# Spreading the gate projections and two branch products through the RWKV stage, and inverting blocks of 32 instead of 16

## The chip, the cores and the metric

The kernel runs on one core of one Trainium2 chip. The metric is the device time of one execution in microseconds (us). TensorE (PE) does the matrix products, VectorE (DVE), ScalarE (ACT) and GpSimd (POOL) the elementwise work; SyncE (SP) and ACT issue most of the DMAs. An engine works through its own queue in the order in which the program was written.

## The reference, cut to what matters

The whole is two transformer-like blocks on 512 latent and 256 context tokens of width 1024. The change lies in the first block's mixer. It has three branches of width 512 (pooling, differential attention, a bidirectional RWKV recurrence), whose products with `w_br` are gated and summed:

```python
w_log = -softplus(-(w0 + einsum('bldr,drc->bldc', tanh(wl), w2))) - 0.5
decay = exp(-exp(w_log)) ...
def wkv_step(S, inp):                      # one token; scanned forwards and backwards
    r, w, k, v, a, b = inp
    sa = einsum('dbhvk,dbhk->dbhv', S, a)
    S = S * w[..., None, :] + sa[..., None] * b[..., None, :] + v[..., None] * k[..., None, :]
    return S, einsum('dbhvk,dbhk->dbhv', S, r)

def merge_branches(branches, gates, w_br, w_out):
    g = sigmoid(gates.reshape(B, L, N_BRANCH, D_MODEL))
    merged = g[:, :, 0] * (branches[0] @ w_br[0])
    for n in range(1, N_BRANCH):
        merged = merged + g[:, :, n] * (branches[n] @ w_br[n])
    return merged @ w_out
```

The kernel does the recurrence in chunks of 128 tokens. That needs the inverse of a unit triangular 128x128 matrix per chunk, head and direction (a matrix I - A, A strictly triangular). It inverts small diagonal blocks row by row on VectorE and joins them by doubling (16 to 32 to 64 to 128) on TensorE, then corrects the result once.

## The kernel before, in words

**Order of the work.** All instructions go through a thin wrapper (`Engine`, so nearly all rows carry line L355, the wrapper's). A class `Clock` keeps a rough model of the engines while the program is written. `weave` (line 1361) takes several generators ("streams"), each with a rank; it runs next the stream whose announced time has come, lowest rank first. If the modelled recent activity of TensorE is under `LOW`, streams of rank 2 go first: these are fillers. What comes out is a fixed order on every engine.

**The first stage** (`phase1`, line 738) weaves four streams: `rwkv_inputs`, `attend` and `rwkv_blocks` of rank 0, and `pools_gates` of rank 2, which ends with the filler `ada_steps` (products with the `ada` weights, matmuls named `ada`). `rwkv_inputs` goes through four column chunks c of the branch. Each ends by transposing the gathered 32x32 blocks (`blkT<-blk`, `rwkv_chunk_inputs`) and putting a job on `todo`; `rwkv_blocks` takes it up. `rwkv_block` (line 1329) inverts two 16x16 blocks of every 32x32 block at a time, in 15 steps i of one multiplication (`blt<-inv,blkT`, 2·i·i elements) and one sum (`inv<-blt`) on DVE. Between steps it yields: for 1 us of modelled TensorE time in chunks 0 to 2 (`PACE`), for none in chunk 3, whose job comes last, beside the end of attention. Two transposes (`blkO`) and four stores to `rw_inv` end it.

**The RWKV stage** (`rwkv`, line 1386) has 24 units and 24 steps (4 column chunks times 6 token chunks). Two generators `units` of rank 1 prepare units, at most `AHEAD` = 3 ahead; two generators `steps` of rank 0, for two column chunks at a time, carry the state S through. `rwkv_unit` loads the operands and `rw_inv` (tile X), makes the masked products (matmuls `m`, tiles Mt, Mh, Ml, Ah, Al), then goes three times through the level loop (line 1488): matmuls `pg`, DVE mask G, matmuls `pT` and `pZ`, DVE additions into TZ (the last turn writes T and has no `pZ`). Then come `pZt`, `pR`, `pf`, and last the pair Zh, Zl. `rwkv_step` does the products `pc`, `pw`, `py` with Rs, Us and S on ACT and DVE between them. `rwkv_out` normalises a finished column chunk and stores it to `rw_out`.

The filler of this stage is `gates` (line 782): 24 projections of the latent tokens (matmuls `gp<-h1l_...`), each in two halves of 12 matmuls of 512 columns, with the weights split into a high part on ACT (`wgh`) and a low part on DVE (`wgl`), then a tanh on ACT and a store to `gates`. Nothing holds it back but its rank.

**The merge stage** (`merge`, line 1110) goes over the branches b = 0, 1, 2. It loads a branch from HBM (`brt<-pooled`, `attended`, `rw_out`), splits it, and for each of 8 output tiles n loads a weight unit (`wr<-w_br`) and a gate (`bgt<-gates`), does 12 matmuls of 512 columns, multiplies by the gate on DVE (`mt`, one buffer; for b = 0 into `mg` itself) and, for b = 1 and 2, adds to `mg` on POOL. Then `mg` is halved and split, and 8 tiles of the `w_out` product follow. Loads of expert weights (`ew<-w_exp`) for the next stage are issued in between on SP.

Of the kernel before, what the change touches and what calls it, by code (L numbers as in the profile page):

```python
# [30 lines left out]
NL, NCX = 512, 256  # L31
# [124 lines left out]
def _tables():  # L156
# [261 lines left out]
class Builder:  # L418
# [288 lines left out]
    def phase1(self, es):  # L707
# [12 lines left out]
        self.d_g = dt("gates", [3, 8, 128, NL])  # L720
        self.d_br = [dt(n, [4, 128, NL]) for n in ("pooled", "attended", "rw_out")]
        self.fac = self.pool(es, "keep1").tile([128, 4, 2, 6, 2], FT, name="fac")
        with ExitStack() as e:
            hl = self.pool(e, "h1l")
# [57 lines left out]
    def gates(self, es, which, tag, ahead, kc, **k):  # L782
# [6 lines left out]
        for b, n in at:  # L789
# [4 lines left out]
            yield self.after(t)  # L794

# [314 lines left out]
    def merge(self, es):  # L1110
# [5 lines left out]
        acc = mp.tile([128, 8, NL], FT, name="mg")  # L1116
        halves = lambda: [wp.tile([128, 4, NL], FR, name=n, tag=n) for n in ("br_hi", "br_lo")]
        for b in range(3):
            bh, bl = halves()
            for c in range(4):  # L1120
                t = wp.tile([128, NL], FT, name="brt", tag="brt")
                nc.scalar.dma_start(t, self.d_br[b][c])
                self.split(bh[:, c], bl[:, c], t)
            for n in range(8):
                t = wp.tile([128, NL], FT, name="bgt", tag="bgt", bufs=3)
                nc.scalar.dma_start(t, self.d_g[b, n])
                (y,) = self.gemm_fm(self.wunit(D["w_br"], (b * 8 + n) * 512 * 128, 4, 128, ring), 0, 4, [(bh, bl, 0, NL)])

                o = acc[:, n] if b == 0 else wp.tile([128, NL], FT, name="mt", tag="mt", bufs=1)
                nc.vector.scalar_tensor_tensor(o, t, 1.0, y, op0=OP.add, op1=OP.mult)  # L1130
                if b:
                    nc.gpsimd.tensor_add(acc[:, n], acc[:, n], o)
                yield
# [37 lines left out]
    def rwkv_inputs(self, es):  # L1171
# [25 lines left out]
        inv = wp.tile([128, 33, 32], FT, name="inv")  # L1197
        nc.gpsimd.memset(inv, 0.0)
        nc.gpsimd.memset(inv[:, :32].rearrange("p i j -> p (i j)")[:, 0::33], 1.0)
# [12 lines left out]
    def rwkv_chunk_inputs(self, c, proj, pp, W, blk, inv):  # L1212
# [102 lines left out]
        A = pp.tile([128, 33, 32], FT, name="blkT", tag="blkT")  # L1315
        nc.vector.transpose(A[:, :32], blk)
# [14 lines left out]

# [1599 lines left out]
```

## Time and profile before

| | us |
|---|---|
| median of 3 runs | 4079.49 |
| lowest and highest | 4067.55 and 4089.53 |
| profiled execution, whole time | 4074.84 |
| its span | 4073.0 |
| PE, DVE, ACT, POOL busy | 3729.5, 2439.1, 1579.8, 530.0 |

A busy time adds up the instructions of an engine; instructions that overlap a little in the pipeline are united in the share. The chain that ended last is 57% PE and 8% DVE. The granted clock of TensorE has two levels, 1.2 and 2.4 GHz, and is given as a share of the higher: 1.00 or 0.50, or a mean of the two over a stretch. A matmul's duration holds its time in the pipeline, so throughput is read from the distance between the starts of neighbouring matmuls. In a row of a timeline, [1.44 <-DVE Rs] means that the engine sat idle for 1.44 us before it, and that DVE's write of Rs ended that.

The stages that the change touches lie at about 115 to 660 us (first stage), 660 to 1344 us (RWKV stage) and 1344 to 1484 us (merge stage: products until 1431 us, then `w_out`).

### The profile page before, as it was taken

How to read it: one execution, taken by the hardware profiler on the slowest of the kernel's cores; microseconds unless marked ns; L12 is line 12 of the kernel's file. 1: busy time of each engine (PE TensorE's matmuls, PEld its weight loads, DVE VectorE, ACT ScalarE, POOL GpSimd, SP SyncE). 2: the span in 40 equal slices, each digit the busy share in tenths (PEclk: the TensorE clock that was granted, in tenths of full speed). 3: DMA queues.
4: the chain of work that ended last, by engine and by line, in shares of the span. 5: the costliest groups of instructions: out<-in, count | busy, mean ns of one | idle time of the engine just before them, and what ended most of it. 6: DMA issues, size and time to landing. Idle time of an engine off the chain costs nothing.

```text
span 4073.0 us, 50718 instructions
## 1 busy us (share of the span) xinstructions
PE 3729.5 (92%) x18620; PEld 2905.8 (71%) x18620; DVE 2439.1 (60%) x4500; ACT 1579.8 (39%) x2765; POOL 530.0 (13%) x750
## 2 busy tenths in 40 slices
PE   8998987998898779999998999899999999999998
PEld 4775435887787667666665887587888887667886
DVE  5577776767776558888874566545323335445444
ACT  3332333332222237666663554223312324434342
POOL 0222211212221221111100000110100100000010
PEclk9998998996556879999999999999999999999999
DMA  5225663321100729998964334411111210012322
GB/s 188 94 94 190 212 226 105 99 95 36 43 27 17 264 76 367 335 340 330 333 256 162 110 122 145 151 32 57 63 63 63 83 63 27 13 42 81 100 93 88
DMA packets 213183, 537.97 MB, mean 132 GB/s; under 512 B 41282, under 2 KB 63459, under 8 KB 186436
## 3 DMA queue, kind: packets, MB, share of 16 engines
q1 hardware_dynamic: 172240, 461.38, 32.8%
q10 hardware_dynamic: 36852, 61.79, 4.4%
q0 software_dynamic: 3840, 11.54, 0.9%
q8 instruction: 148, 2.42, 0.2%
q14 instruction: 103, 0.84, 0.1%
HBM read 486.38 MB, written 48.24 MB: 131 GB/s over the span
## 4 chain that ended last, share of the span: by engine, by line
PE 57%; DVE 8%; ACT 2%; DMA 2%; issue 2%; POOL 1%; another core or an unknown queue 0%; ACTq 0%; SPq 0%; DVEq 0%; POOLq 0%
PE gp L355 33%; PE eg L355 5%; PE ed L355 3%; DVE el L355 2%; PE S L355 2%; PE vp L355 1%; PE eT L355 1%; PE o L355 1%; PE cp L355 1%; PE pc L355 1%; PE fk L355 1%; ACT eh L355 1%; PE py L355 1%; PE hy L355 1%; PE mw L355 1%
## 5 line engine op out<-in xcount | busy, mean ns | idle before, releaser
L355 ACT CAST wh<-wr 128x512 fp32r<-128x512 f32 (+5 forms) x306 | 199.6, 675 | 599.2 <-PE gp L355 538.6
L355 PE MATMUL gp<-h_hi,wh 128*128 128x512 f32 (+1 forms) x1128 | 402.0, 360 | 6.4 <-ACT h_hi L355 3.8
L355 DVE TENSOR_TENSOR el<-ew,eh 128x1024 fp32r<-128x1024 f32 x284 | 354.2, 1273 | 58.4 <-ACT eh L355 56.7
L355 PE MATMUL gp<-h_lo,wh 128*128 128x512 f32 (+1 forms) x1128 | 386.8, 357 | 0.5 <-DVE h_lo L355 0.3
L355 DVE TENSOR_TENSOR wl<-wr,wh 128x512 fp32r<-128x512 f32 (+5 forms) x306 | 228.0, 764 | 245.0 <-ACT wh L355 244.2
L355 PE MATMUL gp<-h_hi,wl 128*128 128x512 f32 (+1 forms) x1128 | 344.1, 357 | 0.0
L355 ACT CAST eh<-ew 128x1024 fp32r<-128x1024 f32 x288 | 292.9, 1048 | 18.8 <-PE ec L355 12.9
L355 PEld LDWEIGHTS gp<-h_hi,wh 128*128 128x128 f32 x1128 | 212.8, 190 | 56.6 <-ACT h_hi L355 7.4
L355 PEld LDWEIGHTS gp<-h_lo,wh 128*128 128x128 f32 x1128 | 213.7, 190 | 34.0 <-DVE h_lo L355 2.3
L355 PEld LDWEIGHTS gp<-h_hi,wl 128*128 128x128 f32 x1128 | 190.5, 191 | 16.7 <-DVE wl L355 0.3
L355 PE MATMUL ada<-wada,adas 128*32 128x512 f32 (+1 forms) x576 | 162.8, 651 | 29.3 <-DMA wada<-ada_w 16.2
L355 PE MATMUL gp<-z_hi,wh 128*128 128x512 f32 (+1 forms) x528 | 187.8, 356 | 0.0
L355 PE MATMUL eg<-el,xg 128*128 128x512 f32 x384 | 161.8, 421 | 27.6 <-DVE el L355 27.4
L355 PE MATMUL gp<-z_lo,wh 128*128 128x512 f32 (+1 forms) x528 | 179.1, 354 | 0.0
L355 PE MATMUL eg<-eh,xg 128*128 128x512 f32 x384 | 176.2, 459 | 0.1
L355 PE MATMUL gp<-z_hi,wl 128*128 128x512 f32 (+1 forms) x528 | 158.8, 355 | 0.0
L355 POOL MEMSET cvb<- 128x1 f32 x170 | 9.6, 98 | 1061.2 <-DVE fg L355 691.4
L355 PE MATMUL gp<-h_lo,wih 128*128 128x256 f32 (+1 forms) x384 | 131.4, 342 | 0.0
L355 PE MATMUL gp<-h_hi,wih 128*128 128x256 f32 (+1 forms) x384 | 128.1, 354 | 0.0
L355 PEld LDWEIGHTS eg<-el,xg 128*128 128x128 f32 x384 | 72.4, 189 | 69.9 <-DVE el L355 50.9
L355 PE MATMUL eg<-ew,xw 128*128 128x512 f32 x256 | 120.2, 592 | 0.0
L355 PEld LDWEIGHTS gp<-z_hi,wh 128*128 128x128 f32 x528 | 99.1, 188 | 22.7
(849 smaller groups left out, 9670.5 us busy)
## 6 DMA issues: line engine op xcount, KB each, us to landing
ew<-w_exp SPq DMA_DIRECT2D x192, 1024.0 KB, 6.8
wada<-ada_w SPq DMA_DIRECT2D x192, 256.0 KB, 4.2
wr<-ffn_up SPq DMA_DIRECT2D x176, 256.0 KB, 2.6
wada<-w_ada_b SPq DMA_DIRECT2D x64, 256.0 KB, 4.3
wg<-w_in_a SPq DMA_DIRECT2D x48, 256.0 KB, 2.6
wi<-w_in SPq DMA_DIRECT2D x48, 256.0 KB, 2.7
wr<-ffn_dn SPq DMA_DIRECT2D x32, 384.0 KB, 3.1
wr<-ffn_dn SPq DMA_DIRECT2D x32, 320.0 KB, 3.3
```

Of the source, the lines that this page charges most:

```text
L355: return f(*a, **k)
```

## The change

Two edits. First, `rwkv_block` inverts each 32x32 block whole, in 31 steps with i·i elements each, and the level loop starts at 32, so that it has two turns instead of three. Second, the filler of the RWKV stage becomes `filler`: the 24 gates, then for the branches 0 and 1 the 16 products that `merge` did, with their loads, splits, gating and (for b = 1) additions; the sum goes to HBM as `merged`. The filler may only go as far as the steps that are done allow: item j of 64 (a gate counts two, a product one) waits until j ≤ 64·(done/24 + 0.1). `merge` loads `merged` (2 MB) and does branch 2 alone, with the addition on DVE and two buffers for `mt`. The latent operand `h1l` moves to the other side of SBUF so that its space can be given to the products.

```diff
-    for i in range(4, 7):                     # _tables: masks of the levels
+    for i in range(5, 7):
-    def gates(self, es, which, tag, ahead, kc, **k):
+    def gates(self, es, which, tag, ahead, kc, pace=None, **k):
-        for b, n in at:
+        for i, (b, n) in enumerate(at):
+            while pace and 2 * i > self.FILL * pace():
+                yield self.later()
+    FILL = 64
+    def filler(self, pace):
+        with ExitStack() as e:
+            yield from self.gates(e, range(self.GATES_A, 24), "g", 2, 4, pace, side="right")
+        self.h1s.close()
+        with ExitStack() as e:
+            yield from self.merge_first(e, pace)
+    def merge_first(self, es, pace):
...
+        feed = Feed(self, wp, "b", [units[i] for i in range(16)], 2)
+        for b in range(2):
...
+            for c in range(4):
+                t = wp.tile([128, NL], FT, name="mbt", tag="mbt")
+                nc.sync.dma_start(t, self.d_br[b][c])
+                yield self.after(t)
+                self.split(bh[:, c], bl[:, c], t)
+            for n in range(8):
+                while 48 + 8 * b + n > self.FILL * pace():
+                    yield self.later()
+                t = wp.tile([128, NL], FT, name="mgt", tag="mgt", bufs=2)
+                nc.sync.dma_start(t, self.d_g[b, n])
+                if b:
+                    a = wp.tile([128, NL], FT, name="mga", tag="mga")
+                    nc.sync.dma_start(a, self.d_mg[:, n])
+                H, L = feed.next()
+                yield max(self.after(H, L, bh, bl), self.room("g"))
+                y = self.ps("mp", "g")
+                for k in range(4):
+                    self.gemm_k([y], H, L, k, [(bh, bl, 0, NL)], k == 0, k == 3)
+                nc.vector.scalar_tensor_tensor(t, t, 1.0, y, op0=OP.add, op1=OP.mult)
+                if b:
+                    nc.gpsimd.tensor_add(t, t, a)
+                nc.scalar.dma_start(self.d_mg[:, n], t)
+                yield
     def merge(self, es):
+        nc.scalar.dma_start(acc, self.d_mg)
-        for b in range(3):
...                                            # the body for b = 2 alone, and:
+            o = wp.tile([128, NL], FT, name="mt", tag="mt")
+            nc.vector.scalar_tensor_tensor(o, t, 1.0, y, op0=OP.add, op1=OP.mult)
+            nc.vector.tensor_add(acc[:, n], acc[:, n], o)
     def rwkv_block(self, c, pp, A, inv):
-        for i in range(1, 16):
-            t = pp.tile([128, 2, 15, 15], FT, name="blt", tag="blt")[:, :, :i, :i]
-            nc.vector.tensor_mul(t, I2[:, :, :i, :i].rearrange("p g m j -> p g j m"), A2[:, :, i, None, :i].to_broadcast([128, 2, i, i]))
-            nc.vector.tensor_reduce(I2[:, :, i, :i], t, op=OP.add, axis=AX.X)
+        for i in range(1, 32):
+            t = pp.tile([128, 31, 31], FT, name="blt", tag="blt")[:, :i, :i]
+            nc.vector.tensor_mul(t, inv[:, :i, :i].rearrange("p m j -> p j m"), A[:, i, None, :i].to_broadcast([128, i, i]))
+            nc.vector.tensor_reduce(inv[:, i, :i], t, op=OP.add, axis=AX.X)
     def rwkv(self, es):
-        self.weave(*gens, (2, self.gates(es, range(self.GATES_A, 24), "g", 2, 4)))
+        self.weave(*gens, (2, self.filler(lambda: done[0] / 24 + 0.1)))
     def rwkv_unit(self, c, n, up, q, P):
-        for lv in (4, 5, 6):
+        for lv in (5, 6):
```

## Rows read from the trace of the kernel before

**Rows 1.** The page's 40 slices of the span: granted clock in tenths.
```profile
PEclk9998998996556879999999999999999999999999
```

**Rows 2.** Stretches: length, busy us (x instructions) by engine, clock, DMA share, GB/s.
```profile
core 0: us, PE busy (x) PEld busy (x) DVE busy (x) ACT busy (x) POOL busy (x), PEclk, DMA share, GB/s
240.00:363.00 123.00, 113.73 (x587) 85.77 (x585) 86.02 (x180) 37.03 (x64) 29.18 (x30) 0.93 0.41 137
363.00:494.00 131.00, 123.93 (x544) 64.08 (x543) 95.32 (x224) 45.60 (x108) 23.10 (x29) 0.97 0.63 214
494.00:606.00 112.00, 100.75 (x427) 46.27 (x425) 87.78 (x211) 38.26 (x91) 21.41 (x20) 0.92 0.67 225
606.00:660.00 54.00, 33.61 (x102) 17.45 (x102) 30.64 (x91) 14.17 (x38) 2.73 (x3) 0.69 0.17 50
...
721.00:906.00 185.00, 173.87 (x1100) 148.63 (x1100) 128.49 (x217) 66.86 (x129) 35.13 (x49) 1.00 0.28 91
906.00:1319.00 413.00, 350.00 (x1927) 328.72 (x1927) 304.60 (x569) 107.58 (x213) 97.09 (x113) 0.61 0.11 35
...
1344.00:1431.00 87.00, 71.74 (x301) 56.96 (x301) 46.48 (x68) 28.23 (x47) 27.28 (x16) 0.93 0.80 279
```

**Rows 3.** Timeline of PE: start us, duration us, engine, instruction, count, idle before.
```profile
898.15 0.40 PE L355 MATMUL gp<-h1l_lo,wgh 128*128 128x512 f32 x1
...
900.48 0.40 PE L355 MATMUL gp<-h1l_hi,wgl 128*128 128x512 f32 x1
...
902.52 0.28 PE L355 MATMUL pR<-T,Al 128*128 128x128 f32 x1
...
903.19 0.28 PE L355 MATMUL pR<-T,Al 128*128 128x128 f32 x1
...
909.40 0.44 PE L355 MATMUL pc<-Rs,Zh 128*128 128x128 f32 x1 [1.44 <-DVE Rs L355]
...
1144.93 0.41 PE L355 MATMUL pR<-T,Al 128*128 128x128 f32 x1
...
1146.21 0.41 PE L355 MATMUL pR<-T,Al 128*128 128x128 f32 x1
```

**Rows 4.** Timeline of DVE: the last write (Zl) of units 1, 8 and 24.
```profile
720.65 1.29 DVE L355 TENSOR_TENSOR Zl<-Zt,Zh 128x512 fp32r<-128x512 f32 x1
...
914.99 1.76 DVE L355 TENSOR_TENSOR Zl<-Zt,Zh 128x512 fp32r<-128x512 f32 x1
...
1318.69 0.69 DVE L355 TENSOR_TENSOR Zl<-Zt,Zh 128x512 fp32r<-128x512 f32 x1 [0.68 <-ACT Zh L355]
```

**Rows 5.** Groups, 640 to 1335 us: busy us, mean ns, idle before and releaser.
```profile
L355 DVE TENSOR_TENSOR G<-pg,levels 128x512 fp32r<-128x512 f32 x72 | 49.2, 686 | 5.6 <-PE pg L355 5.1
L355 DVE TENSOR_TENSOR wgl<-wg,wgh 128x512 fp32r<-128x512 f32 x46 | 37.0, 804 | 50.5 <-ACT wgh L355 50.0 <-PE pZt L355 0.4
```

**Rows 6.** Groups of DVE in the first stage: the block inversion, together and by shape.
```profile
L355 DVE TENSOR_TENSOR blt<-inv,blkT 128x2 f32<-128x2 f32 (+14 forms) x60 | 27.4, 456 | 1.0
L355 DVE TENSOR_REDUCE inv<-blt 128x2 f32<-128x2 f32 (+14 forms) x60 | 19.4, 323 | 1.1
...
L355 DVE TENSOR_TENSOR blt<-inv,blkT 128x450 f32<-128x450 f32 x4 | 4.0, 1008 | 0.0
...
L355 DVE TENSOR_REDUCE inv<-blt 128x30 f32<-128x450 f32 x4 | 2.5, 621 | 0.1
...
L355 DVE TENSOR_TENSOR blt<-inv,blkT 128x128 f32<-128x128 f32 x4 | 1.5, 376 | 0.1
...
L355 DVE TENSOR_REDUCE inv<-blt 128x16 f32<-128x128 f32 x4 | 1.1, 282 | 0.1
```

**Rows 7.** Timeline of the merge stage, PE and DVE.
```profile
1353.11 0.76 PE L355 MATMUL gp<-br_hi,wh 128*128 128x512 f32 x1 [11.44 <-ACT wh L355]
...
1392.15 0.69 DVE L355 SCALAR_TENSOR_TENSOR mt<-bgt,gp 128x512 f32<-128x512 f32 x1 [1.19 <-POOL mg L355]
...
1394.63 0.69 DVE L355 SCALAR_TENSOR_TENSOR mt<-bgt,gp 128x512 f32<-128x512 f32 x1 [1.18 <-POOL mg L355]
```

**Rows 8.** DMA of all queues, 1337 to 1377 us.
```profile
DMA packets 5531, 14.74 MB, mean 368 GB/s; under 512 B 610, under 2 KB 828, under 8 KB 4762
```

More of the change, by code (lines that the diff above doesn't have):

```diff
@@ L720, in phase1 @@
         self.d_g = dt("gates", [3, 8, 128, NL])
+        self.d_mg = dt("merged", [128, 8, NL])
         self.d_br = [dt(n, [4, 128, NL]) for n in ("pooled", "attended", "rw_out")]
@@ L723, in phase1 @@
         with ExitStack() as e:
-            hl = self.pool(e, "h1l")
+            self.h1s = ExitStack()
+            hl = self.pool(self.h1s, "h1l", side="right")
             self.h1l = [hl.tile([128, 8, NL], FR, name=n) for n in ("h1l_hi", "h1l_lo")]
@@ L794, in gates @@
             yield self.after(t)
+    FILL = 64
[6 more added lines that the diff above has]
+    def merge_first(self, es, pace):
+        nc, D = self.nc, self.D
+        wp = self.pool(es, "mgf", side="right")
+        units = D["w_br"].rearrange("(n p k c) -> n p k c", p=128, k=4, c=128)
+        feed = Feed(self, wp, "b", [units[i] for i in range(16)], 2)
+        for b in range(2):
+            bh, bl = (wp.tile([128, 4, NL], FR, name=n, tag=n) for n in ("mb_hi", "mb_lo"))
+            for c in range(4):
[21 more added lines that the diff above has]
+                yield
     def silu_cols(self, name):
@@ L1116, in merge @@
         acc = mp.tile([128, 8, NL], FT, name="mg")
+        nc.scalar.dma_start(acc, self.d_mg)
         halves = lambda: [wp.tile([128, 4, NL], FR, name=n, tag=n) for n in ("br_hi", "br_lo")]
-        for b in range(3):
[L1119 to L1133, printed above, removed]
+        bh, bl = halves()
+        for c in range(4):
+            t = wp.tile([128, NL], FT, name="brt", tag="brt")
+            nc.scalar.dma_start(t, self.d_br[2][c])
+            self.split(bh[:, c], bl[:, c], t)
+        for n in range(8):
+            t = wp.tile([128, NL], FT, name="bgt", tag="bgt", bufs=3)
+            nc.scalar.dma_start(t, self.d_g[2, n])
+            (y,) = self.gemm_fm(self.wunit(D["w_br"], (16 + n) * 512 * 128, 4, 128, ring), 0, 4, [(bh, bl, 0, NL)])
+            o = wp.tile([128, NL], FT, name="mt", tag="mt")
+            nc.vector.scalar_tensor_tensor(o, t, 1.0, y, op0=OP.add, op1=OP.mult)
+            nc.vector.tensor_add(acc[:, n], acc[:, n], o)
+            yield
         m = [halves(), halves()]
@@ L1196, in rwkv_inputs @@
         nc.gpsimd.memset(blk, 0.0)
-        inv = wp.tile([128, 33, 32], FT, name="inv")
+        inv = wp.tile([128, 32, 32], FT, name="inv")
         nc.gpsimd.memset(inv, 0.0)
-        nc.gpsimd.memset(inv[:, :32].rearrange("p i j -> p (i j)")[:, 0::33], 1.0)
+        nc.gpsimd.memset(inv.rearrange("p i j -> p (i j)")[:, 0::33], 1.0)
         thw = wp.tile([128, NT], FT, name="thw")
@@ L1314, in rwkv_chunk_inputs @@
             yield self.later()
-        A = pp.tile([128, 33, 32], FT, name="blkT", tag="blkT")
-        nc.vector.transpose(A[:, :32], blk)
+        A = pp.tile([128, 32, 32], FT, name="blkT", tag="blkT")
+        nc.vector.transpose(A, blk)
         self.todo.append((c, pp, A, inv))
@@ L1390, in rwkv @@
         made, done = [0], [0]
-        self.levels = pp.tile([128, 3, 2, 128], FT, name="levels")
+        self.levels = pp.tile([128, 2, 2, 128], FT, name="levels")
         nc.scalar.dma_start(self.levels, self.D["levels"])
@@ L1494, in rwkv_unit @@
             nc.vector.tensor_mul(dh(G), pg.rearrange("p (d h t) -> p d h t", d=2, h=2),
-                                 self.levels[:, lv - 4, :, None, :].to_broadcast([128, 2, 2, 128]))
+                                 self.levels[:, lv - 5, :, None, :].to_broadcast([128, 2, 2, 128]))
             yield self.after(G)
```

6 lines of the change are left out of this document (1 added, 5 removed).

## The prediction

> **What bounds the kernel now.** I read the page's slices first: TensorE's granted clock is near full everywhere except in three or four slices around 900 to 1350 us [rows 1]. The table of stretches puts numbers to it [rows 2]: up to 906 us the clock is 1.00, from 906 to 1319 us it is 0.61, while PE is shown busy 85% of the time and DVE 74%. The timeline of PE tells what that means [rows 3]. The last matmul of the filler starts at 900.48 us. At the full clock the 11 matmuls of 512 columns up to it are 0.233 us apart, and the seven of 128 columns that begin at 902.52 us are 0.112 us apart. At 1145 us the same kind of 128-column matmul comes every 0.213 us (seven in the listed stretch), 1.9 times as far apart. The clock falls as soon as PE has nothing to do for 1.44 us, at 909.40 us.
>
> So the RWKV stage has two halves. The last writes of units 1, 8 and 24 [rows 4] give 27.8 us per unit while the gates are woven in (7 intervals) and 25.2 us after that (16 intervals), 26.0 us over all 23. In the second half PE is the bound, and only because its clock is low: 1927 matmuls in 16 units [rows 2] are 120 a unit, of which 24 (tile m) run in pairs, so 108 slots, 23.0 us at 0.213 us against 12.1 us at 0.112 us. DVE needs 304.6 / 16 = 19.0 us a unit.
>
> In the first stage PE is filled up with `ada` products. What paces it is a chain over all engines, with DVE busy 269.1 us of 366 us (73%) between 240 and 606 us [rows 2]. The merge stage, 87 us for the products, waits in its second half for POOL: with one buffer, `mt` follows the addition on POOL, one tile every 2.48 us [rows 7].
>
> **The change part by part.**
>
> *The inversion* gets dearer. Now it costs (27.4 + 19.4) / 4 = 11.7 us of DVE a block [rows 6]. From the shapes of 128 and 450 elements the multiplication takes 0.125 us plus 1.96 ns an element, the sum 0.147 us plus 1.05 ns an element. The new block has 31 steps and Σ i² = 10416 elements: 3.9 + 20.4 us and 4.6 + 10.9 us, together 39.8 us, 28.1 us more. Three of the four blocks lie at 240 to 606 us. DVE would hold 269.1 + 84.3 = 353 us of work there; at its present share that is 480 us, at 90% 393 us. The rows show no stretch of this stage above 78%, so I take 86%, as there is idle time between the ops that independent steps can fill: 411 us, **+45 us** (bounds +15 and +76 us: at 93% and 80%). The fourth block stands at the end, beside the last attention rows: DVE is busy 30.6 us of 54 us there [rows 2], so part of its 28.1 us fits: **+20 us** (bounds +8 and +28).
>
> The Trainium skill, page "VectorE: DVE Perf Modes", section on the trn2 errata, gives an fp32 tensor_tensor of N elements (N + 151) / 0.96 ns. The trace differs: 450 elements take 1008 ns [rows 6], not 626. By the page's formula the new multiplications are an estimated 15.7 us a block and not 24.3 us, and the first-stage terms would be smaller by a third; the row decides.
>
> *The level loop* loses a turn: per unit three DVE operations of 0.68 us (one G [rows 5], two additions of the same shape), 2.05 us, and 12 matmuls, 1.3 us at the full clock and 2.6 us at the low one.
>
> *The filler* becomes 24·24 + 16·12 = 768 matmuls of 512 columns, 32 a unit: 7.5 us at the full clock, against 16.8 us a unit now in the first third (72 matmuls) and none later. On DVE it costs two splits of 0.80 us a gate [rows 5], and per product a split and a gating plus 8 splits of branch rows at 0.68 us: 1.6 + 1.1 us a unit. DVE per unit is then 19.0 − 2.05 + 2.7 = 19.7 us. PE's own 96 slots are 10.8 us at the full clock, 20.4 us at the low one. The clock will not stay up all the time: a filler item of 2.8 us comes every 9 us or so, and between items PE waits for DVE, as at 909 us. I take 30% of the own work and 15% of the filler at the low clock: 13.7 + 8.6 = 22.3 us of PE a unit. In the cold half PE has 23.0 us of slots in 25.2 us (91%); at 92%, PE needs 24.2 us. So 24.2 instead of 26.0 us over 23 intervals: **−42 us**. Bounds: 22.5 us a unit (clock nearly always up, DVE at 88%) gives −80 us, 26.0 us gives 0.
>
> The added queue entries are covered. SP gets three loads for each product (weights, gate, partial sum); each waits for a buffer that was freed a product earlier, some 9 us before, so the loads of the units behind it are not held. POOL gets eight additions, beside three units of work a step that leave it idle three quarters of the time [rows 2]. If that cover fails, a late unit load costs its few us on PE.
>
> *The merge* keeps 8 of 24 product tiles. The first matmul comes 9 us into the stage, at 1353.1 us [rows 7], since its weights wait for the end of the RWKV stage; that stays. Eight tiles of 12 matmuls at 0.233 us are 22.4 us, then 3 us for gating, addition and split of the last tile: 35 us. The loads set another limit: `merged` 2 MB, `rw_out` 1, `w_br` 2, gates 2 and the expert weights 7 are 14 MB, and the queues move 14.74 MB in 40 us there now, at 368 GB/s [rows 8]. So I take 40 us instead of 87 us: **−47 us** (bounds −55 and −30, the latter if `merged` arrives behind all else). The POOL chain goes, as DVE does the addition.
>
> Sum: 45 + 20 − 42 − 47 = **−24 us**. The profiled execution takes 4074.84 us, 4.65 us under the median of the three runs. It gives 4050.8 us against itself; with half of that distance I say **4053 us**.
>
> **The rivals.**
>
> *A: the clock stays up and both engines pack* (4000 us). With 18.3 us of PE and 19.7 us of DVE a unit, 22.5 us are possible, −80 us; −50 us in the merge; DVE slots in the first stage hide more, +50 us. For it: in the filled third the clock was 1.00 without a break with PE 94% busy [rows 2]. Against it: there the filler was more than twice as dense.
>
> *B: the filler is spread too thin* (slower, 4140 us). Each item finds PE at the low clock, raises it, and it is lost again before the next. If 60% of the own work and half of the filler run at the low clock, PE needs 10.8·1.54 + 7.5·1.42 = 27.3 us a unit, at 92% 29.7 us, +85 us on the stage instead of −42, and the whole is +62 us. The place is the stage's middle, where the gates ran out before; it decides when a unit needs more than 27 us, that is when over 45% of the own work is cold. For it: one wait of 1.44 us was enough to lose the clock [rows 3]. Against it: an item is 12 long matmuls, and PE had enough own work to hold the clock from 900.5 us until the wait before 909.40 us [rows 3]. The Trainium skill, page "TensorE: Matmul & The Clock Gate", section "HAM oscillation", tells of a kernel whose bursts were each followed by a wait and each began at the low clock; that is B's rule, and the trace agrees with it only at 909 us.
>
> *C: DVE bounds the first stage* (4085 us). At 80% DVE the three blocks cost +76 us and the fourth its whole 28 us; with −42 and −47 the sum is +15 us. For it: the blocks' ops, up to 3 us a step, stand in order before those of the chunk chain. It is "no change", by place a loss.
>
> *D: the change does what it says but the units stay late* (4080 us): the two lanes' chain of Rs, Us and S paces the stage, not PE. Then only the turn of the loop is saved, some −10 us, and 65 − 10 − 47 = +8 us. Against it: matmuls stand back to back at 1145 us [rows 3].
>
> **How the numbers follow.** Forecast (4020 to 4075 us) 0.42, A 0.22, B 0.12, C 0.14, D 0.10. 0.5% of the median is 20 us, about what a measurement of this kernel can tell from no change; faster means under 4059 us, slower above 4100 us. Faster: A and 0.28 of the forecast, 0.50. Same: the rest of the forecast, D and half of C and a little, 0.31. Slower: B and some of C, 0.19. The range takes in most of A, the forecast, C and D, and the nearer part of B: 3980 to 4115 us.
>
> **What would show it.** In the profile after: `blt` and `inv` groups that sum to 159 us, and a first stage that ends some 65 us later (the RWKV stage begins near 725 us, not at 660); G with 48 entries, not 72; the clock between 0.75 and 0.95 throughout the RWKV stage, with filler matmuls until the 22nd step; 24 us between the writes of Zl; no `mg` on POOL, and 40 us between the last store of `rw_out` and the first `w_out` matmul. Wrong would make it: a clock under 0.7 in the middle of the stage (B), DVE over 90% with PE idle in the first stage (C), or a Zl distance that stays at 26 us although the clock is up (D).

## The result and the profile after

The changed kernel takes 4025.22 us (median of 4 runs, 4020.61 to 4028.2) where the kernel before took 4074.44 us beside it: a ratio of 0.9875, 95% interval 0.9852 to 0.9898, 49 us less. The forecast was 4053 us, 24 us less than the profiled execution of before; the sign was right and the size half of what came. The profiled execution of the changed kernel took 4023.89 us, its span is 4022.1 us, 50.9 us under the span before.

The page's slices, DVE's busy share and the granted clock in tenths (against [rows 1]):

```profile
DVE  5597797877877468888874567445423344445343
...
PEclk9998896899888789999999999999999999999999
```

The 6, 5, 5 and 6 of before, from about 916 to 1324 us, are gone from the clock's row; a 6 has come at the end of the first stage. The table of stretches (columns as in [rows 2]) cut at the three later blkT, at the last attention row, at the first Zl, the last store of `rw_out` and the end of the merge products:

```profile
240.00:384.00 144.00, 128.06 (x596) 92.40 (x595) 109.56 (x203) 37.08 (x65) 28.21 (x30) 0.88 0.36 123
384.00:527.00 143.00, 131.68 (x555) 65.75 (x554) 117.92 (x258) 47.21 (x111) 21.16 (x27) 0.92 0.58 195
527.00:657.00 130.00, 106.22 (x426) 50.43 (x426) 111.79 (x257) 41.33 (x102) 20.94 (x20) 0.82 0.54 185
657.00:707.00 50.00, 25.69 (x66) 13.70 (x65) 43.45 (x98) 8.87 (x23) 1.96 (x2) 0.60 0.09 32
...
764.24:1338.08 573.84, 478.94 (x3054) 418.74 (x3053) 427.54 (x800) 193.93 (x376) 146.95 (x172) 0.87 0.31 97
...
1338.00:1380.00 42.00, 29.34 (x108) 22.83 (x109) 24.04 (x36) 14.67 (x24) 0.05 (x1) 0.78 0.87 320
```

The stretch of the kernel before that answers to the fifth line, first Zl to last store of `rw_out`:

```profile
720.65:1343.56 622.91, 534.35 (x3078) 487.00 (x3076) 443.98 (x821) 176.78 (x346) 136.39 (x164) 0.73 0.18 56
```

Groups of DVE in the changed kernel (busy us, mean ns | idle before), against [rows 5, 6]:

```profile
L355 DVE TENSOR_TENSOR blt<-inv,blkT 128x1 f32<-128x1 f32 (+30 forms) x124 | 93.0, 750 | 2.1
L355 DVE TENSOR_REDUCE inv<-blt 128x1 f32<-128x1 f32 (+30 forms) x124 | 62.0, 500 | 1.7
...
L355 DVE TENSOR_TENSOR G<-pg,levels 128x512 fp32r<-128x512 f32 x48 | 32.2, 681 | 0.3 <-PE pg L355 0.2
```

Timeline of DVE: last blkT and last blkO, first Zl (against [rows 4]), the last Us of each lane and the last Zl, the last addition of the merge (against [rows 7]):

```profile
656.80 1.25 DVE L355 STREAM_TRANSPOSE blkT<-blk 128x1024 f32<-128x1024 f32 x1
...
718.74 2.23 DVE L355 STREAM_TRANSPOSE blkO<-inv 128x1024 f32<-128x1024 f32 x1 [1.31 <-DMA rw_inv<-blkO]
...
764.24 1.23 DVE L355 TENSOR_TENSOR Zl<-Zt,Zh 128x512 fp32r<-128x512 f32 x1
...
1289.71 0.41 DVE L355 TENSOR_TENSOR Us<-Ust,pc 128x256 fp32r<-128x256 f32 x1
1290.48 0.69 DVE L355 TENSOR_TENSOR Zl<-Zt,Zh 128x512 fp32r<-128x512 f32 x1 [0.35 <-ACT Zh L355]
...
1295.47 0.42 DVE L355 TENSOR_TENSOR Us<-Ust,pc 128x256 fp32r<-128x256 f32 x1
...
1378.31 0.69 DVE L355 TENSOR_TENSOR mg<-mg,mt 128x512 f32<-128x512 f32 x1
```

Where the time went, stage by stage, from these events in both traces:

| | before | after | difference | predicted |
|---|---|---|---|---|
| first Zl | 720.65 | 764.24 | +43.6 | +65 |
| first to last Zl (23 intervals) | 598.0 | 526.2 | -71.8 | -42 |
| last Zl to the last store of `rw_out` | 24.9 | 47.6 | +22.7 | 0 |
| the rest, the merge stage above all | 2729.4 | 2684.0 | -45.4 | -47 |

The last Zl is a bad end for the stage. In the changed kernel the two lanes end 5.8 us apart and their output rows follow one another; before, they ended 20 us apart and the first lane's rows were done beside the second lane's last unit. Taken together, from the first Zl to the last store, the stage lost 49.1 us, and that is how it is measured below.

### The profile page after: what moved, and what is told of

Its sections match the earlier page's. It is cut to its first block, busy times and chain, and to the rows that moved or that the text cites. A ratio compares the mean times of both kernels' runs of the same rounds, so it can differ in the third digit from the quotient of the medians.

```text
span 4022.1 us, 50169 instructions
## 1 busy us (share of the span) xinstructions
PE 3641.9 (91%) x18332; PEld 2802.5 (70%) x18332; DVE 2487.6 (62%) x4564; ACT 1580.0 (39%) x2765; POOL 510.2 (13%) x742
## 4 chain that ended last, share of the span: by engine, by line
PE 55%; DVE 6%; DMA 2%; ACT 2%; issue 2%; POOL 1%; another core or an unknown queue 0%; ACTq 0%; SPq 0%; DVEq 0%; POOLq 0%
PE gp L355 34%; PE eg L355 5%; PE ed L355 3%; DVE el L355 2%; PE S L355 2%; PE vp L355 1%; PE eT L355 1%; PE o L355 1%; PE cp L355 1%; PE fk L355 1%; ACT eh L355 1%; PE ada L355 1%; PE mw L355 1%; PE hy L355 1%; PE pt L355 1%
## 5 line engine op out<-in xcount | busy, mean ns | idle before, releaser
L355 ACT CAST wh<-wr 128x512 fp32r<-128x512 f32 (+4 forms) x290 | 190.0, 679 | 579.4 <-PE gp L355 544.9
L355 DVE TENSOR_TENSOR el<-ew,eh 128x1024 fp32r<-128x1024 f32 x284 | 354.1, 1273 | 58.8 <-ACT eh L355 56.1
L355 DVE TENSOR_TENSOR wl<-wr,wh 128x512 fp32r<-128x512 f32 (+4 forms) x290 | 216.2, 765 | 241.4 <-ACT wh L355 239.3
L355 PEld LDWEIGHTS gp<-z_hi,wh 128*128 128x128 f32 x528 | 99.1, 188 | 22.7
```

The lines of the kernel that those rows point to most:

```text
L355: return f(*a, **k)
```

## The experiments

"Stage" is the stretch from the first Zl to the last store of `rw_out`, in profiled executions; the lines shown are of the table of stretches. Ratios are to the kernel before, with 95% intervals. One profiled execution stands for a stage, and it scatters: three kernels with the same program in this stage (the changed one and the two of the section on the first stage) took 573.8, 577.7 and 568.3 us, and the last blkT came between 651 and 664 us in the sixteen kernels with blocks of 32.

### The change in two halves, and the turn by itself

**The inversion with two turns, all else as before:**

```diff
-        for i in range(1, 16):
+        for i in range(1, 32):
...
-        for lv in (4, 5, 6):
+        for lv in (5, 6):
```

> The inversion alone: blocks of 32 and two turns of the level loop; filler, gates and merge as in the kernel before. Theory 'clock' (the units' -72 us comes from a filler that lasts through the stage and keeps TensorE's clock up): the stage before the units gets some 44 us longer (first Zl 720.65 to about 764), and 23 intervals give back only the turn's chain, 10 to 25 us; time 4093 to 4108 us beside 4074. Theory 'turn' (the 12 matmuls and 3 DVE operations of a turn are most of the -72): in the cold two thirds 2.6 us of 25.2 us of a unit go, in the filled third 1.3 us, together -45 to -55 us; time 4063 to 4073 us. Both expect no change of the tail and of the merge stage.

```profile
773.15:1345.20 572.05, 493.60 (x2838) 445.04 (x2836) 400.93 (x757) 178.65 (x349) 134.77 (x164) 0.73 0.20 63
```

1.0014 (0.9990 to 1.0038). The first Zl came 52.5 us later, the stage got 50.9 us shorter, with the old filler and at the old clock of 0.73. The theory "turn" fits the stage (its 23 intervals lost 53 us); the run, 4080 us, lies between the ranges of the two theories, and its first Zl came later than the 44 us expected.

**The filler with its products and the short merge, blocks of 16 and three turns:** the other half of the diff.

> The filler alone: paced gates with two branches' products and the short merge, blocks of 16 and three turns as in the kernel before. Theory 'clock': first Zl at 720 us as before, the units give back 72 less 10 to 25 us, the tail costs +23 us, the merge -46 us: -70 to -85 us, 3989 to 4004 us. Theory 'turn': the units give back 17 to 27 us, tail +23, merge -46: -40 to -50 us, 4024 to 4034 us.

```profile
712.91:1364.19 651.28, 546.82 (x3331) 483.08 (x3330) 469.87 (x867) 195.67 (x376) 147.83 (x172) 0.82 0.27 86
```

0.9915 (0.9893 to 0.9938). Both theories fell: the clock rose from 0.73 to 0.82, and still the stage got 28.4 us longer. The gain is all the merge's.

**The third turn put back, empty:**

```diff
-        for lv in (5, 6):
+        for lv in (4, 5, 6):
...
-        low = (...) * 1.0
+        low = (...) * (0.0 if i < 5 else 1.0)
```

> The changed kernel, blocks of 32 inverted on DVE, with a third turn of the level loop put back whole and in its place: 12 matmuls, three DVE operations and their waits, under a mask of zeros, so that it adds nothing to the result. The first stage, the filler and the merge stay. It parts the turn from the inversion. Theory 'engines' (the turn is worth what its operations hold on PE and DVE): the two runs with its parts alone gave +25 us (12 matmuls) and +39 us (three DVE operations) in the 23 intervals, at most 64 us together, the larger of them at least: +39 to +64 us, 4055 to 4090 us. Theory 'chain' (the three hops between PE and DVE, and what they do to the order and the clock, come on top): the 96 us between three turns (621.9) and two (526.2): +85 to +100 us, 4105 to 4130 us.

```profile
773.72:1416.03 642.31, 540.48 (x3327) 476.97 (x3326) 471.43 (x867) 195.16 (x376) 149.09 (x172) 0.83 0.28 87
```

1.0090 (1.0068 to 1.0112): slower than the kernel before. The 23 intervals take 612.8 us, 86.6 more than in the changed kernel: "chain" is right in size. With this kernel the change parts into three steps (spans 4073.0, 4049.9, 4100.5, 4022.1 us):

| step | first Zl | stage | rest | span |
|---|---|---|---|---|
| filler, products, short merge | -7.7 | +28.4 | -43.7 | -23.1 |
| blocks of 32 | +60.8 | -9.0 | -1.2 | +50.6 |
| the turn away | -9.5 | -68.5 | -0.4 | -78.4 |
| sum | +43.6 | -49.1 | -45.4 | -50.9 |

By the ratios of the runs the three steps are -35, +71 and -88 us. Of the -9.5, 4.5 us lie before the last blkT, where both kernels do the same. The -9.0 of the second step has no operation behind it; the stages of both kernels hold the same work (3331 and 3327 matmuls), and it shows how far a profile and an order of the queues move such a number. In the other order, the inversion and the turn first, the filler is worth -57.9 us (4080.0 to 4022.1) and costs the stage 1.8 us instead of 28.4. So the two halves help each other, by 35 us in the profiled spans and by some 22 us in the ratios (0.9875 against 0.9915 and 1.0014).

### What a turn is made of

**Its 12 matmuls alone,** into a tile that nobody reads:

```diff
+            if lv < 6:
+                pX = self.ps("pX", "s")
+                for i in range(3):
+                    for u in range(4):
+                        self.mm(pX[:, u * 128:(u + 1) * 128], Ah[:, u], TZ[:, u])
             yield self.after(G)
```

> The changed kernel with the 12 matmuls of a third turn put back in each unit, into a PSUM tile that nobody reads; no DVE operation, no wait comes with them. It tells which part of a turn makes the 96 us between three turns with the paced filler (621.9 us for 23 intervals) and two (526.2). Theory 'PE bound': 23 x 12 x 0.112 = 31 us at the full clock, over PE's share of 0.88: +35 us, 4058 to 4064 us. Theory 'chain' (what a turn costs is its three hops PE to DVE and back): +0 to +12 us, 4025 to 4037 us. Rival 'density' (more columns keep TensorE's clock up): below +15 us with a granted clock above 0.90 in the stage.

```profile
765.99:1354.38 588.39, 506.30 (x3318) 449.45 (x3317) 431.14 (x800) 195.96 (x376) 148.62 (x172) 0.88 0.29 90
```

0.9929 (0.9906 to 0.9952). PE was busy 27.4 us more, the stage got 14.6 us longer; its 23 intervals 25 us longer (551.3), and by the ratio the run takes 22 us more than the changed kernel: between "chain" and "PE bound", at a clock no higher than 0.88.

**Its three DVE operations alone:** the masking of pg three times more, into a tile that nobody reads.

> The changed kernel with three more DVE operations of 128x512 in each unit (the masking of pg again, three times, into a tile that nobody reads), no matmul. 24 x 2.05 us = 49 us of DVE. Theory 'PE bound': +0 to +12 us, 4025 to 4037 us. Theory 'chain' or 'DVE': the operations stand between pg and the rest of the unit on DVE, so the lanes' chains get longer: +30 to +49 us, 4055 to 4075 us.

```profile
771.86:1366.83 594.97, 489.52 (x3046) 426.92 (x3044) 469.44 (x866) 193.94 (x375) 147.43 (x172) 0.85 0.29 93
```

0.9944 (0.9923 to 0.9965). DVE was busy 41.9 us more, the stage 21.1 us longer, its 23 intervals 39 us (565.4), the run 28 us by the ratio and 4056 us in all, where "chain or DVE" began. Together the parts make 36 of the turn's 68.5 us by the stage, 64 of 87 by the intervals and 50 of 88 by the ratios; what makes the rest of the stage's loss is not shown. In none of these stages is an engine full: PE is busy 82 to 86% and DVE 70 to 79% of the seven stages shown so far.

What the pace hangs on shows in the timeline of DVE. Two units and their steps in the changed kernel; tkl is written at the start of a unit, Zl at its end, Us by the step that uses it (units in the order in which they begin):

```profile
902.76 0.68 DVE L355 TENSOR_TENSOR tkl<-tkp,tkh 128x512 fp32r<-128x512 f32 x1
...
912.22 0.68 DVE L355 TENSOR_TENSOR tkl<-tkp,tkh 128x512 fp32r<-128x512 f32 x1
...
939.50 1.24 DVE L355 TENSOR_TENSOR Zl<-Zt,Zh 128x512 fp32r<-128x512 f32 x1 [0.69 <-ACT Zh L355]
...
943.69 0.42 DVE L355 TENSOR_TENSOR Us<-Ust,pc 128x256 fp32r<-128x256 f32 x1
...
945.93 0.68 DVE L355 TENSOR_TENSOR tkl<-tkp,tkh 128x512 fp32r<-128x512 f32 x1
...
950.32 1.28 DVE L355 TENSOR_TENSOR Zl<-Zt,Zh 128x512 fp32r<-128x512 f32 x1 [0.69 <-ACT Zh L355]
```

Two units are under way at a time, and a third begins when one of them is done. Means over the 24 units of a kernel, in us:

| | start of tkl to end of Zl | end of Zl to the tkl two units on | half the sum | one of 23 intervals |
|---|---|---|---|---|
| before | 45.7 | 7.1 | 26.4 | 26.0 |
| changed | 37.9 | 8.7 | 23.3 | 22.9 |
| empty turn | 46.1 | 7.0 | 26.6 | 26.6 |
| its matmuls alone | 42.1 | 6.4 | 24.2 | 24.0 |
| its DVE operations alone | 41.7 | 6.6 | 24.2 | 24.6 |

The gap between two units hardly changes, and the pace goes with the length of a unit's preparation. A whole turn adds 8.2 us to it, the matmuls alone 4.2 and the DVE operations alone 3.8; here the parts nearly add up. The steps follow: in the changed kernel Us ends 3.4 to 9.0 us after the Zl of its unit in 23 of 24 steps, and from Rst to Us a step takes 5.5 us of the 46 us between two steps of a lane. How much of a unit's length is its own work, and how much is waiting in the queues behind the other unit, the steps and the filler, these runs do not part.

### The spread of the filler

**No pace, 76 and 58 items a stage** in place of 64 (`FILL = 1000`, 76, 58), and **the gates alone in the filler,** all 24 products in the merge stage (`FILL = 48`, the old loop of `merge`):

> The changed kernel without the pace: the filler runs as soon as it finds room, gates first and then the products, so it ends early. Theory 'clock': the filled part is as warm and as slow as the filled third was (27.8 us a unit there), the part after it is cold at 25.2 less 2.6 = 22.6 us a unit at best; the 23 intervals take 15 to 40 us more than the 526 us of the changed kernel; the loads that follow the filler are early again, so the tail of +23 us goes: 4015 to 4045 us. Theory 'turn' (the pace does nothing): the intervals stay at 526 us and the tail goes: 4000 to 4005 us.

> The changed kernel with the pace at 76 items a stage, not 64, so that the last product falls some 4 steps earlier. Theory 'tail' (the last products and the loads behind them stand in the way of the output rows): the 48.4 us between the first lane's last Us and the last store fall to about 40 us, and the cold end of the stage costs little: 4012 to 4020 us. Theory 'pace' (what counts is that items last to the end): the last 100 us of the stage fall to a granted clock of 0.5 to 0.6 and get 15 to 25 us longer, which takes more than the tail gives: 4030 to 4042 us.

> The changed kernel with the pace at 58 items a stage, not 64, so that the last product falls at the last step. Theory 'even' (the longer the filler lasts the better; 76 items a stage gave +23 us, no pace +42 us): 4010 to 4025 us, the 23 intervals at 515 to 526 us. Theory 'optimum' (64 is near the best; thinner items lose the clock, and the last products stand before the output rows): 4030 to 4050 us.

> The changed kernel with only the gates in the filler, paced so that the last of 24 falls where the last product fell, and all 24 products in the merge stage as before. The stage has 192 matmuls of 512 columns less (45 us at the full clock), the merge stage 46 us more. Theory 'pace' (any item that comes evenly keeps the clock up): 23 intervals take 526 - 45 = 481 to 500 us, the tail gets shorter by up to 10 us; 4020 to 4045 us. Theory 'columns' (the thinner filler loses the clock): the granted clock falls to 0.75 to 0.82 and the intervals stay at 520 to 540 us: 4060 to 4085 us.

The stages, one line of each, in this order:

```profile
770.33:1380.22 609.89, 502.95 (x3030) 442.55 (x3028) 435.64 (x797) 191.90 (x372) 144.80 (x172) 0.81 0.29 90
```

```profile
757.65:1357.11 599.46, 495.58 (x3054) 433.77 (x3053) 431.25 (x800) 193.46 (x376) 145.03 (x172) 0.83 0.29 93
```

```profile
762.84:1352.59 589.75, 503.44 (x3040) 439.02 (x3039) 432.54 (x792) 194.64 (x377) 147.23 (x172) 0.85 0.27 84
```

```profile
769.60:1315.01 545.41, 454.96 (x2864) 401.24 (x2863) 404.98 (x763) 182.30 (x355) 136.02 (x164) 0.82 0.22 69
```

| | ratio | interval | stage against 573.8 |
|---|---|---|---|
| no pace | 0.9977 | 0.9965 to 0.9988 | +36.1 |
| 76 | 0.9916 | 0.9893 to 0.9939 | +25.6 |
| 58 | 0.9957 | 0.9943 to 0.9971 | +15.9 |
| gates only | 0.9966 | 0.9951 to 0.9981 | -28.4 |

The pace is worth 42 us (0.9977 against 0.9875), more than either theory of that run had, and 64 is the best of the three: "tail" fell at 76, "even" at 58, and both were slower than their rivals had it. At 58 the last addition of the merge comes 52.1 us after the last store (1352.59 to 1404.68), not 40.2, so the late products also hold up what follows; why the stage itself is 16 us longer at 58 stays open. The gates alone make the stage shorter by 28.4 us and the merge products longer by 45.0 us (85.3 us from the last store to the last addition, at 1400.27). So the 16 products cost the stage 28 of the 45 us that they are long, and the total (4067 us), the clock (0.82) and the intervals (520.9 us) are all where "columns" had them; that the clock is the reason, this run doesn't show.

One comparison parts the spread from the products. The inversion alone and the gates alone both have two turns and 24 gates in the stage and 24 products behind it; in the first nothing paces the gates, in the second the steps do. The stage takes 572.1 us at a clock of 0.73 in the first and 545.4 us at 0.82 in the second, the run 1.0014 and 0.9966. So spreading the gates is worth 27 us in the stage, 20 us over the run, and the 16 products take it back. Whether the higher clock or the more even load brings the 27 us is not shown.

### The order of the queues

58 and 76 items changed the order as well as the pace. One constant of the planner, the time that it reckons for a hop between engines, changes the order alone:

```diff
+        self.clock.HOP = 120.0
         gens = [(0, steps(q)) for q in range(self.LANES)] + ...
+        self.clock.HOP = 150.0
```

> The changed kernel with one constant of the planner altered while it writes the RWKV stage: it reckons 120 ns for a hop between engines, not 150. The same operations, pace and data; only the order in which the two lanes and the filler stand in the queues differs. Theory 'work' (the stage's 526 us follow from its operations, the turn less and the spread of the filler): 521 to 537 us for the 23 intervals, as in the six profiles with the pace at 64 and two turns; 4015 to 4035 us. Theory 'order' (526 us come from one lucky order, in which the units of the two lanes end in close pairs; every edit that changed the order, 58 or 76 items a stage, lost it): the units evenly spaced, 550 to 575 us, 4045 to 4075 us.

> The same with 180 ns for a hop. Theory 'work': 521 to 537 us for the 23 intervals, 4015 to 4035 us. Theory 'order': 550 to 575 us, 4045 to 4075 us, at least in one of the two.

> The kernel before, with 120 ns for a hop while the planner writes the RWKV stage. Theory 'work': 598 us for 23 intervals as it is, give or take 8, 4065 to 4085 us. Theory 'order': the order matters here as well, the intervals move by 15 to 40 us to either side.

> The kernel before, with 180 ns for a hop while the planner writes the RWKV stage. Theory 'work': 590 to 606 us for 23 intervals, 4065 to 4085 us. Theory 'order': the intervals move by 15 to 40 us to either side; if both kernels move as far, the measured -49 us are partly the order's and not the change's.

```profile
762.09:1341.56 579.47, 476.36 (x3053) 414.57 (x3052) 431.13 (x801) 193.70 (x376) 148.71 (x172) 0.88 0.30 96
```

```profile
764.08:1343.36 579.28, 484.22 (x3054) 426.69 (x3053) 429.03 (x800) 193.32 (x376) 144.78 (x172) 0.86 0.31 100
```

```profile
726.24:1353.59 627.35, 524.62 (x3078) 476.28 (x3076) 437.23 (x821) 177.96 (x346) 138.61 (x164) 0.74 0.18 56
```

```profile
721.01:1359.48 638.47, 546.77 (x3078) 499.33 (x3076) 441.19 (x821) 177.26 (x346) 139.11 (x164) 0.70 0.17 55
```

The changed kernel gives 0.9892 (0.9869 to 0.9915) and 0.9873 (0.9849 to 0.9897), the kernel before 1.0024 (1.0004 to 1.0043) and 1.0035 (1.0025 to 1.0045). The order is worth up to 16 us in a stage (638.5 against 622.9), and of the three tried both kernels have the best. The kernel before at 180 ns moved by 13 us in the intervals (611.1), less than "order" had and more than "work". The difference between the kernels is not the order's: any of the three stages of the changed kernel is 43 to 65 us shorter than any of the other. At 120 ns the units do end evenly spaced and the last Zl is late (1313.80, 551.7 us after the first), as "order" said, but the last store follows after 27.8 us, and the stage is as long as at 180 ns, where the last Zl comes after 530.0 us and the store 49.3 us later. Units and tail are one number.

### The first stage

**The fourth block's multiplications done twice:** 24 us of DVE more between the last blkT and the last blkO.

```diff
-            nc.vector.tensor_mul(t, inv[:, :i, :i].rearrange("p m j -> p j m"), ...)
+            for _ in range(2 if c == 3 else 1):
+                nc.vector.tensor_mul(t, inv[:, :i, :i].rearrange("p m j -> p j m"), ...)
```

> The changed kernel with each multiplication of the fourth block's inversion done twice (the same product into the same tile): 24 us more of DVE, all between the last blkT (656.80) and the last blkO (718.74), where DVE is 81% busy. It asks whether work of the fourth block lies on the path, for which the prediction counted 20 us of 28 and of which the traces show nothing (last blkT to the first Zl: 114.4 us before, 107.4 after). Theory 'hidden': the first Zl moves by 0 to 8 us, 4025 to 4033 us. Theory 'on the path now': the cover is used up, 15 to 24 us, 4040 to 4049 us.

```profile
749.51 2.22 DVE L355 STREAM_TRANSPOSE blkO<-inv 128x1024 f32<-128x1024 f32 x1 [0.89 <-DMA rw_inv<-blkO]
...
793.21 1.21 DVE L355 TENSOR_TENSOR Zl<-Zt,Zh 128x512 fp32r<-128x512 f32 x1
```

0.9937 (0.9916 to 0.9958). In this timeline of DVE the last blkO comes 30.8 us later and the first Zl 29.0 us, of which 2.6 us lie before the last blkT (659.39): now the block is on the path. The first Zl follows the last blkO after 43.7 us here, 45.5 us in the changed kernel, 50.7 us with the empty turn (723.02 to 773.72) and 77.1 us with the filler alone (635.85 to 712.91). The last two both have three turns: blocks of 16 left at least 26 us of cover at this place. From the last blkT (605.10 with the filler alone, 661.25 with the empty turn) to the last blkO the larger block takes 31.0 us more, to the first Zl 4.7 us more.

**The multiplication reads inv as it lies, the sum reads across:**

```diff
-            nc.vector.tensor_mul(t, inv[:, :i, :i].rearrange("p m j -> p j m"), A[:, i, None, :i]...)
-            nc.vector.tensor_reduce(inv[:, i, :i], t, ...)
+            nc.vector.tensor_mul(t, inv[:, :i, :i], A[:, i, :i, None]...)
+            nc.vector.tensor_reduce(inv[:, i, :i], t.rearrange("p m j -> p j m"), ...)
```

> The changed kernel with the inversion's multiplication reading inv in the order in which it lies, and the sum reading the products across instead. In the changed kernel the multiplication reads inv across (961 elements: 1849 ns, 1.9 ns an element) and the sum reads in order (1150 ns, 1.1 ns an element). Theory 'read order' (the price an element comes from the operand that is read across, in the operation with two operands alone): the multiplication falls to about 1.1 ns an element, 24.3 us a block to 15 us, the sum stays; 9 us less a block, three of them on the path: -25 to -30 us, 3995 to 4003 us. Rival 'the sum takes it over': its price goes to 1.9 ns an element, no gain, 4020 to 4030 us. Rival 'the broadcast': the multiplication stays at 1.9 ns an element, no gain or a loss, 4020 to 4040 us.

```profile
L355 DVE TENSOR_REDUCE inv<-blt 128x31 f32<-128x961 f32 x4 | 7.7, 1929 | 0.0
...
L355 DVE TENSOR_TENSOR blt<-inv,blkT 128x961 f32<-128x961 f32 x4 | 4.6, 1160 | 0.0
```

0.9858 (0.9816 to 0.9900), no different from the changed kernel. The groups of DVE show the multiplication of 961 elements fall from 1849 to 1160 ns and the sum rise from 1150 to 1929 ns: "the sum takes it over". The second operand of the multiplication, repeated from a row, is read in another order too; the sum has one operand, so its rise is the read's alone.

### The tail

In the changed kernel, ACT and POOL after the last unit:

```profile
1312.84 0.33 ACTq L355 DMA_DIRECT2D rw_out<-yo  x1
1313.30 0.63 ACT L355 ACTIVATE gsq<-ysb 128x512 f32<-128x512 f32 x1 [6.78 <-DMA w_r<-w_r]
...
1338.08 0.33 ACTq L355 DMA_DIRECT2D rw_out<-yo  x1
```

```profile
1311.55 1.26 POOL L355 TENSOR_TENSOR yo<-yo,bg 128x512 f32<-128x512 f32 x1 [2.88 <-DMA bg<-rw_bg]
...
1336.79 1.26 POOL L355 TENSOR_TENSOR yo<-yo,bg 128x512 f32<-128x512 f32 x1 [8.51 <-DMA bg<-rw_bg]
```

The second lane's gsq stands behind the first lane's second yo, and the last yo waits for its bg. **x loaded early** (its buffer below the products' pool, so that its 2 MB don't start at 1310 us), **a buffer of its own for bg** (tag "gbg" for "gsq"), and **both:**

> The changed kernel with the buffer of x (2 MB) made when the gates are done, below the buffers of the products, so that its load is issued near 1115 us and not at 1310 us; all else as in the changed kernel. Theory 'late loads' (the 23 us between the last Zl and the last store of rw_out come from x, constants and expert weights that all start at 1310 us and hold up the small loads of the output rows): most of the 23 us go, 4002 to 4012 us. Rival 'filler at the end' (the last product stands in PE's order between the last step and the transposes of the output rows, and its POOL and ACT work with it): at most 5 us go, 4020 to 4028 us.

> The changed kernel with a buffer of their own for the loads bg of the output rows, which before shared one buffer with gsq. In the changed kernel both lanes end 5.8 us apart (last Us 1289.71 and 1295.47), and the second lane's gsq (1313.30) waits until POOL has used the first lane's second bg (1311.55). Theory 'one buffer': the two outputs stood in series through that buffer; the second gsq starts some 10 us earlier and the last store of rw_out (1338.08) comes 8 to 14 us earlier: 4011 to 4017 us. Rival 'late loads': the second gsq moves but the last bg lands when x, constants, merged and expert weights let it; at most 3 us: 4022 to 4028 us.

> The changed kernel with both changes of the tail: a buffer of its own for bg, and the load of x issued when the gates are done (the partial sums' buffer shares that of the branch rows to make room). Theory 'tail' (buffer and late loads each hold a part of the 23 us): the last store of rw_out comes 36 to 40 us after the first lane's last Us, not 48.4; with -5 us (own buffer) and -6 us (early x) as measured apart: 4010 to 4016 us. Rival 'one wait under the other': once the buffer is gone the load of bg is what is late in both, and the two do not add: 4017 to 4024 us.

ACT with the buffer of its own:

```profile
1298.38 0.63 ACT L355 ACTIVATE gsq<-ysb 128x512 f32<-128x512 f32 x1 [3.41 <-DVE ysb L355]
...
1304.55 0.78 ACT L355 ACTIVATE yo<-ytp,vec 128x512 f32<-128x512 f32 x1 [5.54 <-DMA w_r<-w_r]
...
1324.04 0.33 ACTq L355 DMA_DIRECT2D rw_out<-yo  x1
```

From the first lane's last Us to the last store it is 48.4 us in the changed kernel, 42.6 with x early, 41.0 with the buffer, 35.7 with both (39.6 before; 46.8 and 47.5 in the two kernels of the section above, whose tail is that of the changed kernel). Each cause holds 6 to 7 us in the profile, x far less than "late loads" had, and they add up. With the buffer gsq starts 6.8 us after the last Us (1291.55), not 17.8, but yo then waits for bg until shortly before 1324. Over the whole run 0.9858 (0.9834 to 0.9882), 0.9863 (0.9841 to 0.9884) and 0.9858 (0.9839 to 0.9876) cannot be told from 0.9875: both together may be some 7 us better than the changed kernel, which is not shown.

## Why the prediction was half right

**What held.** The work of the inversion: 93.0 + 62.0 = 155 us where the shapes of [rows 6] gave 159. The merge: 40.2 us from the last store to the last addition, as forecast, and no `mg` on POOL. G has 48 entries. The three blocks in the first stage moved the last blkT by 50.6 us (606.23 to 656.80) where +45 stood, inside the bounds, but two errors offset each other there: DVE held 339 us between 240 and 657 us and not 353, and was busy 81% and not 86%.

**The fourth block, +20, is the step that failed in the first stage.** The way from the last blkT to the first Zl got shorter by 7.0 us (114.4 to 107.4), so 27 us of the forecast are missing there. I looked at how full DVE was around the block and not at when its result was wanted. It was wanted late: with three turns in both kernels the larger block costs 4.7 us on this way, and the doubled block shows that the cover is now used up. A thinner filler ahead of the first Zl (-6.6 on this way) and a turn less in the first unit (-5.0) took off the rest, and neither was in my sum. That blocks of 32 by themselves moved the first Zl by 60.8 us, near the +65, is luck: 56.1 us before the last blkT and 4.7 behind it, where 45 and 20 stood.

**The units' term came out near its size for the wrong reason.** -42 was to be compared with -49.1, units and tail together. It is a sum over PE alone: 96 slots for 108. At its own rates the 12 slots of the turn make some -43 us, and the filler nothing. With the inversion first, the runs have -50.9 for the turn and +1.8 for the filler (-27 for spreading the gates, +28 for the products); with the filler first, -68.5 and +28.4. But PE's slots alone do not set the pace. Put back alone, the 12 matmuls, by that sum worth 43 us, cost 14.6 us of stage, and the three DVE operations, by that sum worth nothing, 21.1 us. It goes with the length of a unit's preparation, to which both add some 4 us. The filler alone raised the clock from 0.73 to 0.82 and made the stage 28.4 us longer, with 45 us of products more in it; the turn alone made it 50.9 us shorter at 0.73.

The clock itself came out better than forecast. Of the matmuls recorded between the first Zl and 1310 us some 17% of the stage's own and 11% of the filler's began at the low level, where 30% and 15% stood; over stretches of 40 us it was 0.66 to 1.00 and not 0.75 to 0.95. With these shares the sum would give 22.4 us a unit and -83 us, with -71.8 measured in the intervals and +22.7 in a tail that I had put at nothing. So the -42 is near by offsetting errors.

**The rivals.** D was right that PE alone does not set the pace, and named the wrong chain: the steps with Rs, Us and S wait for their units, and the turn lies in the units. A chain of the steps would have left the turn its -10 us. B's sign is what the filler has with three turns, without B's low clock.

The page "TensorE: Matmul & The Clock Gate" of the Trainium skill, section "HAM oscillation", which I had put beside B, tells of bursts that begin at the low clock. Here 14 of the 74 bursts of the filler in the changed kernel's stage did (filler matmuls that start within 1 us of one another counted as one burst), so the trace agrees with that rule for a fifth of them; in the kernel before it was none.

**Readings and sums of the prediction that are wrong.** A wait of 1.44 us was not by itself enough to lose the clock. Between 664 and 909 us the kernel before kept 1.00 through longer waits of PE, here with the filler around them:

```profile
677.59 0.50 PE L355 MATMUL gp<-h1l_hi,wgh 128*128 128x512 f32 x1 [2.02 <-ACT gt L355]
...
697.99 0.50 PE L355 MATMUL gp<-h1l_hi,wgh 128*128 128x512 f32 x1 [1.64 <-ACT gt L355]
```

What differs at 909 us is that the filler had ended at 900.48 us. The clock was not 1.00 all the way up to 906 us either: [rows 2] has 0.69 from 606 to 660 us. And rival B's terms, 65 + 85 - 47, make +103 us and not +62, so its time would have been some 4180 us.

**The queue entries were costed at nothing,** and that was wrong in one place that was not on the list. Not SP's loads in the middle of the stage, but the pools at its end: the products' pool kept the room of x until 1310 us, and lanes in step met at one buffer. That is 6 to 7 us each.

**The sum.** -24 against -51 is 21 us in the first stage and 7 in the units and their tail, less 2 in the merge.

## What to carry to other kernels

Where two interleaved preparations set the pace and no engine is full, ask how long one of them is from its first operation to its last: here a loop turn was worth more than the busy time that it freed on any engine, and putting an empty turn back measured it. Ask which chain holds the operation that goes, and which one waits. An engine that runs at a low clock is not thereby the bound: ask what the stage does when the clock rises, with the same work in it. And ask of added work when its result is first wanted, before you ask how full its engine is.

## What the hardware showed that I had not expected

A DVE operation in fp32 that reads an operand across, with 128 bytes from element to element in the product and 124 in the sum, took 1.9 to 2.0 ns an element, and 1.2 ns when it read in order, both for the product of two tensors (1849 and 1160 ns for 961 elements) and for the sum (1929 and 1150 ns). This mends a sentence of the prediction: the formula (N + 151) / 0.96 of the Trainium skill's page "VectorE: DVE Perf Modes" gives 1158 ns for 961 elements, so it holds for the read in order; what the rows differed by was the read across. The Trainium skill's page "SBUF — State Buffer" states a cause that would do this, in the note on cachelines of its section "Door 1: The DMA port swizzle": each access that crosses into a new line of 16 bytes pays a penalty. The two rows agree with it.

The granted clock of PE over a stage said little of its length where the work differed: 0.73 went with 622.9 and with 572.1 us, 0.82 with 651.3, 609.9 (0.81) and 545.4 us. With nearly the same work, two turns and the gates alone, 0.73 went with 572.1 us and 0.82 with 545.4 us.
